# A decoder block on one NeuronCore: the transfers that form the weights' block sums move from SyncE's queue to GpSimd's

## The chip, the cores and the metric

The kernel runs on one core of one Trainium2 chip. It has five engines, each with a queue of its own that it works through in order: TensorE (PE; its weight loads are shown as PEld), VectorE (DVE), ScalarE (ACT), GpSimd (POOL) and SyncE (SP). Transfers are started by an instruction in the queue of SP, ACT or POOL; the 16 DMA engines of the core then carry them out. An instruction waits on semaphores at the head of its queue, and whatever stands behind it in that queue waits with it.

The metric is the device time of one launch in microseconds, the median of the runs.

## What is computed

The reference is one decoder block: conditioning from `c`, a combined input projection, a chunked gMLP branch and a sparse-attention branch, gates, an output projection, then a SwiGLU feed-forward layer and a final RMSNorm. The change touches the feed-forward layer:

```python
mod = jax.nn.silu(c) @ w_ada + b_ada
shift1, scale1, gate1, shift2, scale2, gate2 = [m[:, None, :] for m in jnp.split(mod, 6, axis=-1)]
...
h2 = rms_norm(x, norm2_g) * (1.0 + scale2) + shift2
f_g, f_u = jnp.split(h2 @ w_ffn_in, 2, axis=-1)
x = x + gate2 * ((jax.nn.silu(f_g) * f_u) @ w_ffn_out)
```

512 positions, a model width of 1024, a hidden width of 2816, all in float32.

## The kernel before

A float32 product is made of three TensorE products of high and low parts (`mm3`, L51). High parts come from ScalarE, low parts from VectorE as the difference. So each weight block that arrives from device memory costs work on both engines before TensorE can use it.

The two feed-forward projections use Strassen's scheme in Winograd's form: a product of 2x2 blocks takes seven block products, with sums and differences of blocks on both sides. For the first projection (`w_ffn_in`) the sums are made on chip, by VectorE. For the second (`w_ffn_out`) the sums of weight blocks are made in device memory by the DMA engines: four tensors `wsum1` to `wsum4`, each of 1280 x 512, hold them (L274). A sum is formed by a plain copy of one block into `wsum` and then an accumulating transfer that adds another block to it. `wsum_steps` (L292) makes the steps. The rows are cut in five row blocks of 256 (`NZ = 5`), and for each of them there are six steps in a chain:

1. copy a block into wsum1 and another into wsum3 (two transfers);
2. add a block to wsum1 and another to wsum3 (two transfers);
3. copy wsum1 into wsum2;
4. add a block to wsum2;
5. copy wsum2 into wsum4;
6. add a block to wsum4.

Each transfer has 512 KB. In all there are 20 plain copies and 20 accumulating ones. Before the change the plain ones are issued from SP (L307), the accumulating ones from POOL (L305), since only that queue is used for accumulation. Row blocks 0 and 1 are interleaved step by step, then 2 and 3, and block 4 comes alone.

The first projection is a loop over 20 iterations, q from -2 to 17 (L1623), with 84 matmuls of 128x256 each. `s_issue(q + 2)` (L1626) puts two loads of `w_ffn_in` (tile `raw`, L1298) into SP's queue, two iterations ahead; their buffers are those of earlier loads, so SP waits there until VectorE has read the old content. `s_prep(q + 1)` splits and sums the blocks of the next iteration on ScalarE and VectorE (L1324 to L1355). `wstep()` is called twice in each iteration (L1669, L1697) and emits the next entry of the list of steps, or nothing where the entry is None. There are 40 such calls; the list has 24 steps for row blocks 0 to 3 without a gap and then the six of block 4 with a None after each, 36 entries.

In iterations q = 1 to 8, `last_mod` (L1522) forms gate2 beside all this: in each odd one, two slices of `w_ada` (tile `mraw`, L205) are loaded on SP's queue behind that iteration's raw loads, into a pair of buffers that VectorE has just finished with; at the end of each iteration VectorE multiplies and adds one of them into `acc` (L175, L177). VectorE works in order, so what it has to do for the next iteration stands behind that instruction.

POOL has the load of gate2's bias (`gate2b`, L1470) ahead of the loop. The next thing behind the accumulating transfers is the load of the final norm's gain (`fng`, L1774), in the second projection, and at the end four small row statistics (L1235).

The second projection (`zprod`, L1732) reads weight blocks through SP (L92): blocks of `w_ffn_out` for the first product, then wsum1, wsum2, blocks of `w_ffn_out`, wsum3, wsum4 and again `w_ffn_out`. A read of wsum waits for the transfer that completed it.

The order within each engine's queue is the order of the program text (`manual_schedule`, L34); a framework adds the semaphores where one instruction needs another's result.

Of the kernel before, what the change touches and what calls it, by code (L numbers as in the profile page):

```python
# [28 lines left out]
def block_kernel(ctx: ExitStack, tc: tile.TileContext, x, positions, w_ada, b_ada, w_in,  # L29
# [3 lines left out]
    T, V, A, P, SY = nc.tensor, nc.vector, nc.scalar, nc.gpsimd, nc.sync  # L33
# [240 lines left out]
    wsum = {n: dram.tile([NZ * 256, 512], F32, name=f"wsum{n}") for n in (1, 2, 3, 4)}  # L274
# [17 lines left out]
    def wsum_steps():  # L292

        def step(c, *moves):
            o = slice(256 * c, 256 * c + 256)

            def fn():
                for n, add, src in moves:
                    if isinstance(src, tuple):
                        k = KZ[src[0]][2 * c] * 128  # L300
                        src = w_ffn_out[k:k + 256, 512 * src[1]:512 * src[1] + 512]
                    else:
                        src = wsum[src][o]
                    if add:
                        P.dma_start(wsum[n][o], src, accum_op=OP.add)  # L305
                    else:
                        SY.dma_start(wsum[n][o], src)  # L307
            return fn

        parts = [[step(c, *m) for m in (  # L310
            ((1, 0, (0, 0)), (3, 0, (0, 1))), ((1, 1, (0, 1)), (3, 1, (1, 1))), ((2, 0, 1),), ((2, 1, (1, 1)),),
            ((4, 0, 2),), ((4, 1, (1, 0)),))] for c in range(NZ)]
        return ([fn for c in (0, 2) for two in zip(parts[c], parts[c + 1]) for fn in two] +
                [fn for one in parts[4] for fn in (one, None)])

    wsteps = wsum_steps()

    def wstep():
# [1268 lines left out]
    for half in range(2):  # L1587
        o = slice(half * 256, (half + 1) * 256)
# [214 lines left out]
    for h in range(2):  # L1803
        hi, lo = get(W_FO[h])
        for tk in range(4):
            o = (Z[h] if tk < 2 else Z[2 + h])[tk % 2]
# [31 lines left out]
    for tk in range(2):  # L1838
        for z in range(2) if tk else (None,):
            c = ALL if z is None else slice(256 * z, 256 * z + 256)  # L1840
            o = Z[1][0] if z is None else (Z[1][1][:, :256], last[:, :256])[z]
            for n_, w in enumerate(ch):
                zmm(o, "S4", 2 + n_, tk, w, c, False, n_ == 2)
            n = c.stop - c.start
# [62 lines left out]
```

## Time and profile before

| | |
|---|---|
| median of 3 runs | 831.83 us (831.74 to 833.28) |
| profiled execution | 831.31 us |
| its span | 829.5 us |
| mean granted TensorE clock | 0.996 |
| TensorE busy | 810.3 us, 98% |
| VectorE busy | 684.5 us, 83% |
| DMA, mean over the span | 167 GB/s |

The span runs from the first to the last instruction; the execution's time holds a little more around it. Busy time of PE is that of pipelined matmuls with modelled ends, so in a stretch without waits it is 100% and says little; the number of matmuls that start in a window of 10 us says more. "q1" is the ring of SP's transfers, "q0" that of POOL's. The DMA share is the mean busy share of the 16 DMA engines and can pass 1 where packets of two rings overlap. "us to landing" runs from the issue of a transfer to its completion.

### The profile page before, as it was taken

The page shows a single profiled execution, that of the slowest core. Times are in us where ns is not written, and L with a number is a line of the kernel's source. Part 1 is how long each engine was busy: PE and PEld are TensorE (multiplying, and loading weights), DVE is VectorE, ACT ScalarE, POOL GpSimd, SP SyncE. Part 2 cuts the span into 40 slices and gives each one's busy share as a digit, 9 for nine tenths or more (in the row PEclk, how much of TensorE's full clock was granted, in tenths as well). Part 3 has the DMA queues.
Part 4 walks back from the last instruction along what each step waited for, and adds up shares of the span by engine and source line. Part 5 has one row for each costly group of instructions (what it writes and reads, how often), then busy time and mean ns, then how long its engine had stood idle before and what let it go on. Part 6 is the DMA issues. An engine that isn't in the chain of part 4 may idle for free.

```text
span 829.5 us, 12872 instructions
## 1 busy us (share of the span) xinstructions
PE 810.3 (98%) x4920; PEld 723.6 (87%) x4920; DVE 684.5 (83%) x1167; ACT 427.0 (51%) x730; POOL 126.7 (15%) x121
## 2 busy tenths in 40 slices
PE   7999999999999999999999999999899999999995
PEld 6889889988888888988888899999899999888784
DVE  7989788798899558886697869899699888897676
ACT  6674444323322236665536586555355556666543
POOL 2060032362353411000000001001000000000001
PEclk9999999999999999999999999999999999999999
DMA  9974352423345652057531409899998863556533
GB/s 296 310 203 118 102 178 77 118 87 101 124 137 176 197 178 77 26 157 243 185 102 50 154 28 257 222 271 295 254 265 208 199 162 125 178 189 195 177 129 126
DMA packets 108477, 138.46 MB, mean 167 GB/s; under 512 B 6480, under 2 KB 77136, under 8 KB 108256
## 3 DMA queue, kind: packets, MB, share of 16 engines
q1 hardware_dynamic: 99872, 120.24, 45.7%
q0 software_dynamic: 7824, 16.59, 10.4%
q8 instruction: 38, 0.62, 0.3%
q10 hardware_dynamic: 720, 0.82, 0.3%
q14 instruction: 23, 0.19, 0.1%
HBM read 135.26 MB, written 23.07 MB: 191 GB/s over the span
## 4 chain that ended last, share of the span: by engine, by line
PE 50%; DVE 18%; DMA 6%; ACT 2%; issue 2%; POOL 0%; POOLq 0%; ACTq 0%; DVEq 0%
PE R L53 6%; PE R L54 6%; PE R L55 6%; DMA mraw<-in_w_ada_dram 6%; PE pfo L55 3%; PE pfo L53 3%; PE pfo L54 3%; DVE acc L177 3%; DVE sco L713 2%; DVE m L709 2%; PE pb L53 2%; PE pb L55 2%; PE pb L54 2%; DVE lo L116 2%; PE po L54 2%
## 5 line engine op out<-in xcount | busy, mean ns | idle before, releaser
L112 ACT ACTIVATE hi<-raw 128x1024 fp32r<-128x1024 f32 (+2 forms) x103 | 107.0, 1040 | 105.3 <-PE pfo L55 34.3
L116 DVE TENSOR_TENSOR lo<-raw,hi 128x1024 fp32r<-128x1024 f32 (+2 forms) x67 | 81.1, 1214 | 29.1 <-ACT hi L112 28.9
L116 POOL TENSOR_TENSOR lo<-raw,hi 128x1024 fp32r<-128x1024 f32 x29 | 73.3, 2531 | 127.9 <-ACT hi L112 122.2
L53 PE MATMUL pb<-h,hi 128*128 128x512 f32 (+1 forms) x192 | 74.6, 389 | 0.0
L54 PE MATMUL pb<-h,hi 128*128 128x512 f32 (+1 forms) x192 | 74.0, 385 | 0.0
L55 PE MATMUL pb<-h,lo 128*128 128x512 f32 (+1 forms) x192 | 74.0, 385 | 0.0
L54 PE MATMUL pfo<-lo,za 128*128 128x512 f32 (+1 forms) x146 | 56.3, 385 | 0.3 <-DVE lo L116 0.3
L55 PE MATMUL pfo<-hi,za 128*128 128x512 f32 (+1 forms) x146 | 56.2, 385 | 0.0
L53 PE MATMUL pfo<-hi,za 128*128 128x512 f32 (+1 forms) x146 | 56.1, 385 | 0.0
L177 DVE SCALAR_TENSOR_TENSOR acc<-mraw,cols,acc 128x512 f32<-128x512 f32 x49 | 39.6, 808 | 18.9 <-DMA mraw<-in_w_ada_dram 17.9
L53 PE MATMUL R<-tb,hi 128*128 128x256 f32 x160 | 45.0, 281 | 2.9 <-ACT R L1670 2.1
L53 PE MATMUL R<-tb,sx 128*128 128x256 f32 x160 | 45.3, 283 | 0.9 <-ACT R L1657 0.8
L54 PE MATMUL R<-tb,sx 128*128 128x256 f32 x160 | 45.1, 282 | 0.0
L55 PE MATMUL R<-tb,sx 128*128 128x256 f32 x160 | 45.0, 281 | 0.0
L55 PE MATMUL R<-tb,lo 128*128 128x256 f32 x160 | 44.9, 281 | 0.0
L54 PE MATMUL R<-tb,hi 128*128 128x256 f32 x160 | 44.7, 279 | 0.0
L305 POOL DMA_DIRECT2D wsum<-in_w_ffn_out_dram x20 | 17.8, 908 | 172.7 <-DMA wsum<-wsum 115.3
L55 PEld LDWEIGHTS pb<-h,lo 128*128 128x128 f32 x192 | 36.0, 187 | 7.3
L54 PEld LDWEIGHTS pb<-h,hi 128*128 128x128 f32 x192 | 36.0, 188 | 6.9
L53 PEld LDWEIGHTS pb<-h,hi 128*128 128x128 f32 x192 | 36.0, 188 | 6.9
L1235 POOL TENSOR_TENSOR sm<-sm,mhalf 128x1 f32<-128x1 f32 x8 | 5.3, 662 | 217.6 <-DVE sm L1234 217.6
L54 PE MATMUL pav<-lo,h 128*128 128x256 f32 x128 | 35.8, 279 | 0.0
(373 smaller groups left out, 2643.6 us busy)
## 6 DMA issues: line engine op xcount, KB each, us to landing
raw<-in_w_ffn_in_dram SPq DMA_DIRECT2D x44, 512.0 KB, 6.5
raw<-in_w_in_dram SPq DMA_DIRECT2D x40, 512.0 KB, 3.8
mraw<-in_w_ada_dram SPq DMA_DIRECT2D x28, 512.0 KB, 4.0
wsum<-in_w_ffn_out_dram POOLq DMA_DIRECT2D x20, 512.0 KB, 9.3
raw<-wsum SPq DMA_DIRECT2D x20, 512.0 KB, 3.7
raw<-in_w_ffn_out_dram SPq DMA_DIRECT2D x18, 512.0 KB, 3.8
s<-in_w_ada_dram SPq DMA_DIRECT2D x30, 256.0 KB, 5.6
wsum<-in_w_ffn_out_dram SPq DMA_DIRECT2D x10, 512.0 KB, 8.6
```

The source lines that it names most:

```text
L53: T.matmul(o, wh, rh, start=start, stop=False, **kw)
L54: T.matmul(o, wh, rlo, start=False, stop=False, **kw)
L55: T.matmul(o, wlo, rh, start=False, stop=stop, **kw)
L112: A.activation(hi[:, :m], e["raw"][:, :m], AF.Copy)
L116: e["lo"].tensor_sub(lo[:, :m], e["raw"][:, :m], f(hi[:, :m]))
L177: V.scalar_tensor_tensor(o, w, cs[:, j:j + 1], o, op0=OP.mult, op1=OP.add)
L305: P.dma_start(wsum[n][o], src, accum_op=OP.add)
L709: V.max(m8s[i], sco[i])
L713: V.match_replace(out=sco[i], in_to_replace=m8s[i], in_values=sco[i], imm_value=TAKEN)
L1235: P.tensor_tensor(r2[:, tk:tk + 1], r2[:, tk:tk + 1], mhalf[:, :1], op=OP.pow)
```

## The change

```diff
--- before.py
+++ after.py
@@ -304,14 +304,14 @@
                     if add:
                         P.dma_start(wsum[n][o], src, accum_op=OP.add)
                     else:
-                        SY.dma_start(wsum[n][o], src)
+                        P.dma_start(wsum[n][o], src)
             return fn
 
         parts = [[step(c, *m) for m in (
             ((1, 0, (0, 0)), (3, 0, (0, 1))), ((1, 1, (0, 1)), (3, 1, (1, 1))), ((2, 0, 1),), ((2, 1, (1, 1)),),
             ((4, 0, 2),), ((4, 1, (1, 0)),))] for c in range(NZ)]
-        return ([fn for c in (0, 2) for two in zip(parts[c], parts[c + 1]) for fn in two] +
-                [fn for one in parts[4] for fn in (one, None)])
+        order = [fn for c in (0, 2) for two in zip(parts[c], parts[c + 1]) for fn in two] + parts[4]
+        return [fn for k in range(0, len(order), 3) for fn in order[k:k + 3] + [None]]
 
     wsteps = wsum_steps()
```

The 20 plain copies are issued from POOL's queue, as the accumulating transfers are. The order of the steps is the same; a None now follows every third step, so that the list has 40 entries for the 40 calls of `wstep()`. The line numbers of the rest of the kernel do not move.

## The prediction

> **What bounds the kernel now.** I read the page first, then busy time in 10 us windows over the first FFN projection, then who waited for whom where the windows show a hole, then the two issue queues and the DMA engines in that stretch.
>
> ```profile
> span 829.5 us, 12872 instructions
> PE 810.3 (98%) x4920; PEld 723.6 (87%) x4920; DVE 684.5 (83%) x1167; ACT 427.0 (51%) x730; POOL 126.7 (15%) x121
> ```
>
> TensorE has work for 98% of the span, so a change that touches no matmul can only give back, or add to, the few places where TensorE stands still. The profiled execution took 831.31 us in all, 1.8 more than its span and 0.5 less than the median of the runs, 831.83. The windows have one such place in the FFN projection (columns: stretch, its length, busy time and starts of PE, PEld, DVE, ACT and POOL, granted clock, DMA share, GB/s):
>
> ```profile
> 580.00:590.00 10.00, 10.00 (x86) 9.89 (x84) 5.44 (x8) 2.84 (x6) 0.00 (x0) 1.00 1.11 234
> 590.00:600.00 10.00, 7.11 (x47) 6.72 (x47) 7.41 (x10) 3.99 (x6) 1.27 (x2) 0.83 0.81 296
> 600.00:610.00 10.00, 9.20 (x78) 9.00 (x77) 9.59 (x13) 6.45 (x12) 0.50 (x1) 1.00 1.05 221
> ```
>
> A full window, like the first, has 86 matmul starts; 590 to 610 has 47 + 78, so 47 starts are missing, at 10/86 = 0.116 us each 5.5 us. Part of it is idle, part the granted clock of 0.83. The DMA engines are full or nearly so, 0.81 to 1.11. The waits between 574 and 606 us name the cause:
>
> ```profile
> DVE acc L175 <- DMA mraw<-in_w_ada_dram: 6.4, 1, 6.4
> ACT sx L1335 <- DMA raw<-in_w_ffn_in_dram: 3.1, 1, 3.1
> PE R L53 <- ACT R L1670: 2.1, 1, 2.1
> ```
>
> VectorE stood 6.4 us for a slice of w_ada (mraw) and everything it prepares for TensorE came late. Why was that load late? These are SP's issues, then POOL's, around it (start, duration, what; "x4" is four issues):
>
> ```profile
> 497.82 2.55 SPq L307 DMA_DIRECT2D wsum<-in_w_ffn_out_dram  x4
> ...
> 532.61 2.18 SPq L1298 DMA_DIRECT2D raw<-in_w_ffn_in_dram  x2
> ...
> 542.58 2.18 SPq L1298 DMA_DIRECT2D raw<-in_w_ffn_in_dram  x2
> ...
> 553.29 1.59 SPq L1298 DMA_DIRECT2D raw<-in_w_ffn_in_dram  x2
> ...
> 562.50 2.18 SPq L1298 DMA_DIRECT2D raw<-in_w_ffn_in_dram  x2
> 564.73 3.02 SPq L307 DMA_DIRECT2D wsum<-in_w_ffn_out_dram  x4
> 573.48 1.59 SPq L1298 DMA_DIRECT2D raw<-in_w_ffn_in_dram  x2
> 576.81 1.19 SPq L205 DMA_DIRECT2D mraw<-in_w_ada_dram  x2
> ...
> 602.92 1.03 SPq L205 DMA_DIRECT2D mraw<-in_w_ada_dram  x2
> ```
>
> ```profile
> 487.11 0.57 POOL L1470 DMA_DIRECT2D gate2b<-in_b_ada_dram  x1
> 506.75 1.93 POOL L305 DMA_DIRECT2D wsum<-in_w_ffn_out_dram  x2 [19.07 <-DMA wsum<-in_w_ffn_out_dram]
> ...
> 572.97 0.88 POOL L305 DMA_DIRECT2D wsum<-in_w_ffn_out_dram  x1 [18.22 <-DMA wsum<-in_w_ffn_out_dram]
> ...
> 577.18 0.88 POOL L305 DMA_DIRECT2D wsum<-in_w_ffn_out_dram  x1 [0.42 <-issue]
> ...
> 677.25 0.88 POOL L305 DMA_DIRECT2D wsum<-in_w_ffn_out_dram  x1 [19.24 <-DMA wsum<-wsum]
> ```
>
> SP's queue is paced by compute: a raw load waits for VectorE to free its buffer, so SP passes two iterations in 562.50 - 542.58 = 19.9 us, and the plain copies of wsum, standing between the loads, are paced with them. Each second iteration from q=1 to q=7 has a burst of four loads, two raw and two mraw. At 573 four accumulating transfers started together with such a burst. The issues between 572 and 578 us, with median time to landing, show who lost:
>
> ```profile
> wsum<-in_w_ffn_out_dram POOLq DMA_DIRECT2D x4, 512.0 KB, 11.2
> raw<-in_w_ffn_in_dram SPq DMA_DIRECT2D x2, 512.0 KB, 13.8
> mraw<-in_w_ada_dram SPq DMA_DIRECT2D x2, 512.0 KB, 16.1
> ```
>
> **The change, part by part.** What the steps are and what they depend on stays. Twenty plain copies leave SP's queue and join POOL's; empty slots are spread through the list of steps. No instruction on TensorE, VectorE or ScalarE moves.
>
> *The even spread: nothing.* A slot of the list sets only where a step stands in its queue, and a queue is paced only by waits. In the order of the changed kernel POOL's 40 issues of wsum stand in one row between gate2b and fng, and wait for nothing but landings of transfers of POOL's own queue. Nothing there waits for TensorE, VectorE or SP. So POOL runs through all of them at the pace of their landings, from gate2b at 487.7 us on. The pacing of SP is lost, not gained.
>
> *What the wsum transfers cost the DMA engines.* Queues and issues between 490 and 700 us:
>
> ```profile
> q1 hardware_dynamic: 25326, 35.19, 49.5%
> q0 software_dynamic: 5458, 10.53, 32.2%
> ...
> raw<-in_w_ffn_in_dram SPq DMA_DIRECT2D x37, 512.0 KB, 6.6
> wsum<-in_w_ffn_out_dram POOLq DMA_DIRECT2D x20, 512.0 KB, 9.3
> wsum<-in_w_ffn_out_dram SPq DMA_DIRECT2D x10, 512.0 KB, 8.6
> wsum<-wsum SPq DMA_DIRECT2D x10, 512.0 KB, 7.1
> mraw<-in_w_ada_dram SPq DMA_DIRECT2D x8, 512.0 KB, 10.3
> raw<-in_w_ffn_out_dram SPq DMA_DIRECT2D x3, 512.0 KB, 3.6
> ```
>
> q0 is POOL's: 0.322 x 210 us / 20 = 3.4 us of all engines for an accumulating transfer. q1 is SP's: 0.495 x 210 / 68 issues = 1.5 us for a plain one. The whole wsum work is 20 x 3.4 + 20 x 1.5 = 98 us, the same before and after.
>
> *Over how long it is spread.* Before: 497.8 to 677.25 + 9.3 = 686.6, 189 us, a share of 0.52. After: three blocks (two pairs of column blocks and a single one), each with six steps in a chain, copy, add, copy, add, copy, add, so by the median landings 8.6 + 9.3 + 7.1 + 9.3 + 7.1 + 9.3 = 50.7 us a block, 152 us in all, done at about 640. The share becomes 98/152 = 0.64. A plain copy from POOL's queue into device memory does not occur before; I take SP's landing times for it. Bounds from the extremes of the two lines:
>
> ```profile
> L307 SPq DMA_DIRECT2D wsum<-wsum x10: 473/522/3041, 524.9 to 671.0; - x10
> ...
> DMA to landing us min/median/max: 5.5/8.2/10.7
> ...
> L305 POOL DMA_DIRECT2D wsum<-in_w_ffn_out_dram x20: 872/881/1307, 506.8 to 677.3; - x20
> ...
> DMA to landing us min/median/max: 6.6/9.3/14.9
> ```
>
> All at minimum: 3 x (3 x 5.5 + 3 x 6.6) = 109 us, share 0.90. All at maximum: 3 x (3 x 10.7 + 3 x 14.9) = 230 us, share 0.43. I take the medians: they were measured beside the same loads.
>
> *What meets it.* In the stretch with mraw loads two iterations carry four raw and two mraw loads, 6 x 1.5 = 9.1 us in 19.9, a share of 0.46. Before: 0.52 + 0.46 = 0.98, just full, which is why one bad coincidence cost 6.4 us. After: 0.64 + 0.46 = 1.10. The stretch runs from the first burst at 532.6 to the last mraw's landing, 602.92 + 10.3 = 613, and the chain covers all of it: 80 us x (0.64 - 0.52) = 9.6 us more work than the engines have time for. Who waits for it? In the rows of 572 to 578 the additions kept their pace and the loads took the delay. So the loads wait, VectorE waits for them, and I book the whole 9.6 us there, in pieces at the four bursts, the largest where the four additions of the second block stand (about 488 + 51 + 9 = 548 to 560 us, on the burst of about 553).
>
> The Trainium skill, "DMA: Bandwidth & Descriptors", section "Queues, rings and completion order", says that each DMA engine takes turns between the queue rows with work, a packet at a time. That speaks against the change: a copy that stood in line with SP's loads now competes with them from another row. The rows of 572 to 578 agree, as far as loads losing to additions go; whether plain copies from POOL press as hard, no row here shows.
>
> *From VectorE to TensorE.* 6.4 us of waiting became 5.5 us lost, so the slack between them is 0.9 us and the wait of before has used it. From there each us passes through: the loss becomes 5.5 + 9.6 = 15.1 us.
>
> *SP's side: nothing.* SP is freed of twenty issues, at 473 to 3041 ns each. Its loads wait for buffers that VectorE frees, and a load behind a copy had an iteration, 10 us, to land. Even 1 us gained per burst would not undo an overload. Without that cover the gain is bounded by the copies' share of a burst's wait, which is rival A.
>
> *POOL's side: nothing.* Twenty more issues at 881 ns, 18 us, on an engine idle until the load of fng:
>
> ```profile
> 709.93 0.58 POOL L1774 DMA_DIRECT2D fng<-in_final_norm_g_dram  x1 [31.79 <-PE R L55]
> 711.09 8.30 SPq L92 DMA_DIRECT2D raw<-wsum  x3
> ```
>
> Behind the waiting additions stand only further additions, then fng, then row statistics of the end. The first sum is read at 711.09; with the chain at its longest (488 + 230 = 718) only the fourth sum would be late, and that is read last of the four. Were this cover gone, SP would stand before that read and TensorE with it.
>
> *Sum:* 831.3 + 9.6 = 840.9 on the profiled execution; the median lies 0.5 above it. The engines cannot be overbooked for long without the landings, and so the chain, stretching; for that I take a little off: 840 us.
>
> **The rivals.** A, *the coincidence goes* (faster). Before, additions start at 572.97 and a burst at 573.48 because both follow SP's rhythm; a free chain may miss the bursts, or slow itself down (by maximum landings its share falls to 0.43). Then the 5.5 us come back: 831.3 - 5.5 = 825.8. Against it: a chain with a share of 0.64 leaves no burst alone. The Trainium skill, "SBUF — State Buffer", section "SBUF: two separate sides", has another way to a slow chain: VectorE in certain modes locks POOL out of writing descriptors. In the quoted line 20 issues took 872 to 1307 ns beside a busy VectorE, so no run here shows such a lock.
>
> B, *only the issuer changes* (no change): all transfers share the same engines, the chain stretches by as much as it is pressed, and the waiting stays near 6 us: 831.5. For it: the work of 98 us is the same. Against: the share of 0.98 before. The same page on DMA, section "Issuing engines are not separate DMA queues", of the Trainium skill says that issuing from several engines saves no more than issue time; by that alone nothing would change, but here the queue also set the pace.
>
> C, *the chain runs at its shortest* (slower still): share 0.90, for 109 us from 488 to 597, over the bursts from 532.6 to 597: 64 us x (0.90 - 0.52) = 24 us, less the 16 us x 0.52 = 8 that the rest of the stretch is spared, so 16 more: 847. For it: two column blocks run side by side, so a stage can start before the last landing of the one before. Against: minimum landings are those of an idle machine.
>
> That the change does not do what it says, an even spread, is my forecast itself.
>
> **How the numbers follow.** Forecast 0.60, C 0.13, A 0.19, B 0.08. About 0.2% (1.7 us) is what a measurement of this kernel can tell from no change. Slower holds the forecast and C, 0.73; faster is A, 0.19; same is B, 0.08. The time is the forecast's, 840. The range must leave out no more than 2 in 10: 827 to 848 takes in B and C and the upper edge of A. The forecast's own range is 835 to 846: half the overload to one and a half times it.
>
> **What would show it.** Right: no wsum issue on SP; POOL's first at about 488 and its last before 650; VectorE's waits for mraw at three or four bursts, together 12 to 18 us; missing matmul starts in several windows between 540 and 615, none after; from 660 on the DMA share lower than before. Wrong: POOL's issues reaching past 690 (something paces them), waits for mraw under 6 us (A), loads landing in 9 us beside four additions (the engines do not favour POOL's), or TensorE waiting after 711 for a wsum load.

## The result, and the profile after

The changed kernel takes 838.22 us (median of 4 executions, 837.22 to 839.22), the kernel before 831.91 us beside it (4 executions, 831.74 to 833.28): a ratio of 1.0072, with a 95% interval of 1.0055 to 1.0090. It is slower by 6.3 us; 840 had been forecast. The profiled execution took 839.22 us.

First the head of the page of the changed kernel:

```profile
span 837.4 us, 12858 instructions
...
PE 812.6 (97%) x4920; PEld 725.5 (87%) x4920; DVE 685.0 (82%) x1167; ACT 426.3 (51%) x730; POOL 136.8 (16%) x141
```

The same 4920 matmuls in a span that is 7.9 us longer: TensorE stands still more. Where, the windows over the first FFN projection show (stretch, its length, busy time and starts of PE, PEld, DVE, ACT and POOL, granted clock, DMA share, GB/s):

```profile
540.00:550.00 10.00, 10.00 (x87) 10.00 (x85) 5.55 (x9) 4.11 (x8) 2.68 (x3) 1.00 1.05 348
550.00:560.00 10.00, 4.96 (x34) 4.66 (x34) 6.53 (x9) 2.32 (x5) 1.41 (x2) 0.81 1.11 235
560.00:570.00 10.00, 8.00 (x54) 7.60 (x53) 3.72 (x6) 2.65 (x8) 2.03 (x3) 0.85 1.02 334
570.00:580.00 10.00, 8.65 (x73) 8.66 (x74) 9.79 (x14) 5.80 (x9) 0.80 (x2) 1.00 1.03 233
580.00:590.00 10.00, 9.52 (x80) 9.32 (x80) 9.90 (x15) 5.62 (x13) 3.47 (x5) 1.00 0.85 209
...
600.00:610.00 10.00, 8.55 (x72) 8.35 (x71) 8.30 (x11) 3.99 (x6) 1.41 (x2) 1.00 1.12 284
610.00:620.00 10.00, 9.19 (x77) 8.99 (x76) 9.55 (x14) 6.34 (x12) 0.87 (x1) 1.00 0.96 275
```

Against 86.5 starts in a full window (86 or 87 in the windows shown as full), the six short ones have 34 + 54 + 73 + 80 + 72 + 77 = 390 where 519 would be full: 129 missing, at 0.116 us 14.9 us. Before it was 5.5 us in two windows. The waits of the changed kernel between 495 and 715 us (who waited, for what: us in total, times, longest) say what stood behind it:

```profile
DVE acc L175 <- DMA mraw<-in_w_ada_dram: 10.5, 2, 7.1
...
DVE raw L1327 <- DMA raw<-in_w_ffn_in_dram: 8.2, 3, 6.3
...
PE R L53 <- ACT ps L1677: 6.5, 2, 5.0
...
ACT hi L1335 <- DMA raw<-in_w_ffn_in_dram: 3.8, 1, 3.8
...
PE R L53 <- ACT R L1670: 2.6, 1, 2.6
...
PE R L53 <- ACT R L1657: 2.0, 3, 0.8
```

TensorE waited 6.5 + 2.6 + 2.0 = 11.1 us. In windows of 1 us the granted clock was 0.50 behind its longest wait, until 563 us, and TensorE worked for 4.7 us of that: 4.7 x (1 - 0.50) = 2.4 us more. Together 13.5 of the 14.9 us; the rest was not followed. Above TensorE's waits stand VectorE and ScalarE waiting for loads, and not for mraw alone: the raw loads of `w_ffn_in` were as late. In the kernel before VectorE waited 6.7 us for mraw in this stretch and for no raw load.

The first matmul of the second projection tells how late the loop ended. One row from the view of the tile pfo in the changed kernel (duration min/median/max in ns, first and last start):

```profile
L53 PE MATMUL pfo<-hi,za x146: 277/395/400, 720.0 to 829.4; 128*128 128x512 f32 x134, 128*128 128x256 f32 x12
```

Before, the same row goes from 710.9 to 820.3. The loop ends 9.1 us later, and the whole second projection is shifted by the same 9.1 us. The span grows by 7.9 only: the tail behind the last of these matmuls is 829.5 - 820.3 = 9.2 us before and 837.4 - 829.4 = 8.0 after. That 1.2 us goes with the queue: the tail is 9.2 us in all four kernels here that leave the copies on SP, and 7.9 to 8.1 in the six that have them on POOL with sums and whole pieces (changed, paced, one and five blocks at a time, mraw loaded once, a wait between pairs). In the two kernels that leave the sums out it is 10.5 and 10.7, so the queue is not all of it; what it is stays open.

Now the queue. The transfers of wsum in the changed kernel (issue time in ns, first and last start):

```profile
L305 POOL DMA_DIRECT2D wsum<-in_w_ffn_out_dram x20: 869/894/985, 494.5 to 627.1; - x20
...
L307 POOL DMA_DIRECT2D wsum<-in_w_ffn_out_dram x10: 557/894/914, 487.6 to 587.7; - x10
L307 POOL DMA_DIRECT2D wsum<-wsum x10: 505/518/529, 502.2 to 621.7; - x10
```

All 40 are POOL's, from 487.6 to 627.1 where they had gone to 677.3. Nothing of the list's even spread shows in them. POOL's issues where the first pair of row blocks ends and the second begins (the last addition of blocks 0 and 1, four copies of blocks 2 and 3, then the first and the last of four additions):

```profile
532.19 0.89 POOL L305 DMA_DIRECT2D wsum<-in_w_ffn_out_dram  x1 [1.66 <-DMA wsum<-wsum]
532.76 2.58 POOL L307 DMA_DIRECT2D wsum<-in_w_ffn_out_dram  x4
543.71 0.92 POOL L305 DMA_DIRECT2D wsum<-in_w_ffn_out_dram  x1 [8.37 <-DMA wsum<-in_w_ffn_out_dram]
...
550.79 0.89 POOL L305 DMA_DIRECT2D wsum<-in_w_ffn_out_dram  x1 [0.92 <-DMA wsum<-in_w_ffn_out_dram]
```

and SP's issues in the same stretch:

```profile
532.57 2.17 SPq L1298 DMA_DIRECT2D raw<-in_w_ffn_in_dram  x2
534.79 2.30 SPq L205 DMA_DIRECT2D mraw<-in_w_ada_dram  x2
542.53 19.51 SPq L1298 DMA_DIRECT2D raw<-in_w_ffn_in_dram  x4
```

The first step of blocks 2 and 3 waits for nothing of blocks 0 and 1, so it starts while the last additions of these are still moving: a seam at which POOL's ring holds ten transfers almost without a pause. The burst of 532.6 to 535 meets the first half of it, the two raw loads behind 542.53 the second. In the view of the DMA issues between 542 and 546 us (KB, median us to landing), and of the rings between 548 and 562 us (packets, MB, share of 16 engines' time):

```profile
raw<-in_w_ffn_in_dram SPq DMA_DIRECT2D x2, 512.0 KB, 23.8
```

```profile
q0 software_dynamic: 1038, 2.14, 79.1%
q1 hardware_dynamic: 1072, 1.33, 32.4%
```

A raw load took 23.8 us here, against 6.6 in the median before and 13.8 for the two at the hole of before. And the two rings moved nearly the same number of packets, the pieces in which the profile counts what a ring moves, 1038 and 1072: the engines serve them in turn, one packet each. POOL's packet (q0) takes 0.791 x 16 x 14 us / 1038 = 171 ns, SP's (q1) 0.324 x 224 / 1072 = 68 ns. So while both rings were filled, SP's ring had less than a third of the time: 1.33 MB in 14 us, one load of 0.524 MB in 5.5 us. The loop needs one in 3.3 us where mraw is loaded (six in 19.9 us) and one in 5 us elsewhere.

### The profile page after: what moved, and what is told of

Read it like the earlier page. It is cut to its first block, busy times and chain, and to the rows that moved or that the text cites. A ratio compares the mean times of both kernels' runs of the same rounds, so it can differ in the third digit from the quotient of the medians.

```text
span 837.4 us, 12858 instructions
## 1 busy us (share of the span) xinstructions
PE 812.6 (97%) x4920; PEld 725.5 (87%) x4920; DVE 685.0 (82%) x1167; ACT 426.3 (51%) x730; POOL 136.8 (16%) x141
## 4 chain that ended last, share of the span: by engine, by line
PE 83%; DVE 6%; DMA 6%; ACT 2%; issue 1%; SPq 0%; POOL 0%; POOLq 0%; DVEq 0%
PE pb L53 9%; PE pb L55 9%; PE pb L54 9%; PE R L53 5%; PE R L54 5%; PE R L55 5%; PE pfo L55 3%; PE pfo L53 3%; PE pfo L54 3%; DMA raw<-in_w_ffn_in_dram 3%; PE pav L54 2%; PE pav L53 2%; PE pav L55 2%; PE pgb L53 2%; PE pgb L54 2%; PE pgb L55 2%
## 5 line engine op out<-in xcount | busy, mean ns | idle before, releaser
L53 PEld LDWEIGHTS R<-tb,hi 128*128 128x128 f32 x160 | 30.7, 192 | 7.0 <-ACT ps L1677 6.9
```

What stands on the lines that cost most here:

```text
L53: T.matmul(o, wh, rh, start=start, stop=False, **kw)
```

## The experiments

All times are medians, each compared with the kernel before on the same chip; over the chips used, the median of the kernel before lay between 831.2 and 832.1. Edits are shown against the changed kernel where nothing else is said. "Loop end" is the first start of pfo as above, from the profiled execution; for a wait between pairs and for no additions that execution lay 2.4 and 2.7 us above the median, so their loop ends are late by about as much.

| run | us | ratio to before, 95% interval | loop end |
|---|---|---|---|
| before | 831.9 | | 710.9 |
| changed | 838.22 | 1.0072 [1.0055, 1.0090] | 720.0 |
| list alone | 833.47 | 1.0019 [1.0009, 1.0030] | 712.3 |
| paced by ScalarE | 827.33 | 0.9966 [0.9934, 0.9997] | 706.2 |
| one block at a time | 824.39 | 0.9914 [0.9892, 0.9936] | 705.8 |
| mraw loaded once | 837.13 | 1.0073 [1.0051, 1.0094] | 717.7 |
| five blocks at once | 861.41 | 1.0364 [1.0340, 1.0388] | 741.7 |
| a wait between pairs | 831.92 | 1.0004 [0.9989, 1.0018] | 715.1 |
| one at a time, copies on SP | 830.18 | 0.9978 [0.9963, 0.9994] | 707.8 |
| mraw earlier, kernel before | 837.35 | 1.0070 [1.0052, 1.0088] | 716.2 |
| no additions | 832.51 | 1.0010 [0.9994, 1.0027] | 713.6 |
| five at once, no additions | 855.36 | 1.0283 [1.0234, 1.0333] | 734.1 |
| short pieces | 1219.33 | 1.4653 [1.4627, 1.4680] | 719.2 |
| five at once, short pieces | 1216.72 | 1.4634 [1.4612, 1.4656] | 720.9 |

### The list alone, the copies left on SP

```diff
-                        P.dma_start(wsum[n][o], src)
+                        SY.dma_start(wsum[n][o], src)
```

> The new list with its even gaps, plain copies left on SP. Theory (the loss comes from the wsum work losing SP's pace and being pressed into 147 us over the mraw bursts): the copies keep SP's pace, the chain even ends some 20 us later than before, so no loss: 827 to 832 us. Rival (the even list itself is what hurts): near 838. Rival (the ring the copies come from is what hurts): also 827 to 832, so this run does not tell the ring from the pace.

1.5 us slower than before. It keeps one hole, later than that of before; its window, and the wait behind it:

```profile
610.00:620.00 10.00, 5.76 (x36) 5.48 (x36) 6.38 (x9) 3.18 (x6) 0.00 (x0) 0.83 0.67 247
```

```profile
DVE acc L177 <- DMA mraw<-in_w_ada_dram: 7.4, 1, 7.4
```

So the list moves the coincidence to another burst and does not remove it. The other half, the old list with the copies on POOL, would be the changed kernel itself: POOL issues nothing between its 40 transfers of wsum, and the two lists have them in the same order. The loss is that of the queue.

### On POOL, but paced

```diff
         fn = wsteps.pop(0) if wsteps else None
         if fn:
+            mark = ffn[0].tile([128, 1], F32, name="mark", tag=f"mark{len(wsteps)}", bufs=1)
+            seen = ffn[0].tile([128, 1], F32, name="seen", tag="seen", bufs=1)
+            A.activation(mark, f(onesr[:, 0:1]), AF.Copy)
+            P.tensor_tensor(seen, mark, mhalf[:, :1], op=OP.pow)
             fn()
```

> As the changed kernel, all wsum transfers on POOL, but in front of each step POOL waits for a one-column ScalarE instruction of that iteration, so the steps really are spread over the 20 iterations. Theory (pace): wsum's share of the DMA engines falls from 0.67 to about 0.5, the additions no longer overlap in fours, VectorE's waits for mraw under 4 us together: 826 to 832 us. Rival (ring: plain copies from POOL's ring press SP's loads whatever their pace): still 836 to 840.

827.33 us, with executions from 825.2 to 828.2 and three at 833.9 to 834.7; the profiled one, 825.49, is of the first kind. The issues of wsum now run from 509.8 to 703.3, and VectorE waits 3.1 us for loads where it had waited 18.7. All copies are POOL's here too, so POOL's ring as such does not cost: what it had lost was the pace.

### One row block at a time

```diff
-        order = [fn for c in (0, 2) for two in zip(parts[c], parts[c + 1]) for fn in two] + parts[4]
+        order = [fn for one in parts for fn in one]
```

> As the changed kernel, all wsum transfers on POOL and without any wait for compute, but the five row blocks one after another, not two interleaved. Theory (how much wsum work stands in the DMA engines at a time): the chain takes 5 x 40 to 50 = 200 to 250 us, a share of 0.4 to 0.5, at most two additions at once: 826 to 831 us, faster than before. Rival (ring): 836 to 840, since every copy still comes from POOL. Rival (phase, only the coincidence of bursts with additions counts): anything from 826 to 838.

824.39 us: this beats both kernels, by 0.9% and 1.6%. It has no added wait; a chain of dependent transfers leaves pauses by itself. Its additions, its windows at the place of the changed kernel's hole, and the rings between 532 and 566 us:

```profile
L305 POOL DMA_DIRECT2D wsum<-in_w_ffn_out_dram x20: 869/890/982, 493.8 to 668.0; - x20
```

```profile
550.00:560.00 10.00, 10.00 (x87) 10.00 (x86) 9.57 (x12) 6.53 (x13) 2.55 (x4) 1.00 0.72 223
560.00:570.00 10.00, 10.00 (x86) 10.00 (x86) 9.24 (x16) 4.50 (x9) 0.91 (x1) 1.00 1.05 320
```

```profile
q0 software_dynamic: 1207, 3.56, 47.4%
q1 hardware_dynamic: 4214, 5.18, 45.3%
```

The same two rings in the changed kernel, same stretch:

```profile
q0 software_dynamic: 2202, 5.72, 72.0%
q1 hardware_dynamic: 3253, 3.75, 35.6%
```

SP's loads need six times 0.524 MB in 19.9 us, 5.4 MB in these 34 us. One block at a time lets through 5.18, the changed kernel 3.75. Over the whole chain, though, POOL's share here is that of the kernel before: 98 us of work in the 188 us from 487.7 to the last landing at about 675, 0.52. A mean share cannot tell these apart. That only the phase counts, which transfer happens to meet which burst, is not excluded by this run alone.

### mraw loaded once

```diff
-        if k % 2 == 0:
+        if k == 0:
```

Here six of the eight mraw loads are left out; VectorE multiplies the first two slices again.

> As the changed kernel, but only the first two of the eight mraw slices of w_ada are loaded and all eight multiply-adds read those two: six loads and the right value of gate2 are left out. Theory (overload in the stretch with mraw loads): 0.67 + 0.31 leaves the engines just not full, most of the loss goes: 827 to 832 us. Rival (the raw loads of w_ffn_in are hurt as much, mraw is only the messenger): 834 or more, with VectorE and ScalarE waiting for raw.

837.13 us: the loss stays although six of the 24 loads of that stretch are gone. Two windows and the first two of VectorE's waits for loads:

```profile
550.00:560.00 10.00, 5.87 (x37) 5.67 (x38) 7.69 (x10) 2.66 (x4) 1.66 (x3) 0.77 1.11 238
560.00:570.00 10.00, 7.03 (x50) 6.77 (x48) 3.96 (x8) 3.66 (x8) 2.30 (x3) 0.84 1.04 305
```

```profile
DVE raw L1327 <- DMA raw<-in_w_ffn_in_dram: 9.7, 3, 6.0
...
DVE acc L175 <- DMA mraw<-in_w_ada_dram: 6.4, 1, 6.4
```

The later, smaller holes of 600 to 620 are gone, and the big one stands. By the prediction's arithmetic the engines are no longer full without those loads, 0.64 + 4 x 1.5 / 19.9 = 0.94; so an overload of the whole stretch with mraw loads is not the mechanism. The first mraw burst is still there, and VectorE's 6.4 us are a wait for it, so its part in the big hole stays open in this run; in the next run the loss begins before any mraw load.

### All five row blocks at once

```diff
-        order = [fn for c in (0, 2) for two in zip(parts[c], parts[c + 1]) for fn in two] + parts[4]
+        order = [fn for same in zip(*parts) for fn in same]
```

> As the changed kernel, but all five row blocks side by side: ten copies, then ten additions, then five of each and five of each again. Theory (what counts is how much wsum work stands in POOL's ring without a pause, against the 10 to 13 us that a load has to land): 10 x 1.5 + 10 x 3.4 = 49 us without a pause from 488 on; the loads land one in about 7 us while two are needed in 10; 845 to 860 us, and the loss lies at 505 to 590, much of it before the first mraw load at 535. Rival (only the stretch with mraw loads can be hurt): the chain is nearly done when that stretch begins, 828 to 838.

861.41 us. The windows from 500 us on have 82, 73 and 32 starts, so the loss begins long before the first mraw load of this kernel at 545. Rings and raw loads between 500 and 540 us:

```profile
q0 software_dynamic: 3078, 7.02, 82.1%
q1 hardware_dynamic: 3015, 3.01, 26.8%
...
raw<-in_w_ffn_in_dram SPq DMA_DIRECT2D x4, 512.0 KB, 18.7
```

Again nearly equal numbers of packets (310 and 310 between 512 and 516 us alone), 171 ns for POOL's (0.821 x 640 / 3078) and 57 ns for SP's. 3.01 MB in 40 us is one load in 7.0 us, where the loop needs one in 5 even without mraw. This run gave the rule its plain form: not how much POOL moves counts, but how long its ring is never empty.

### A wait between the pairs

```diff
+        def after_landing(c, fn):
+            def both():
+                t = ffn[0].tile([128, 1], F32, name="seen", tag="seen", bufs=1)
+                P.dma_start(t, wsum[4][256 * c:256 * c + 128, 0:1])
+                fn()
+            return both
+
+        parts[2][0], parts[4][0] = after_landing(1, parts[2][0]), after_landing(3, parts[4][0])
```

> As the changed kernel, but between two pairs of row blocks POOL waits until the last addition of the pair has landed (it issues a 512-byte read of wsum4 in between). The chain gets some 15 us longer, 162 instead of 147. Theory (standing work): the ten transfers that stood together at 530 to 566 (two additions, four copies, four additions, 26 us) become at most eight, 20 us: the loss falls to a half or less, 829 to 834 us. Rival (mean share of the DMA engines, the sum of the prediction): 98/162 = 0.60 instead of 0.67, 835 to 838.

831.92 us, 6.3 us better than the changed kernel for two reads of 512 bytes whose only use is to hold POOL until the earlier pair has landed. One hole remains, 20 us later, from four copies at 545.4 and the four additions behind them, on the burst of 553:

```profile
570.00:580.00 10.00, 5.17 (x27) 4.97 (x26) 3.41 (x6) 1.33 (x2) 2.30 (x3) 0.66 1.03 315
580.00:590.00 10.00, 7.95 (x65) 7.54 (x65) 9.90 (x13) 6.94 (x13) 1.94 (x3) 1.00 0.92 239
```

Against one block at a time, 824.39, the changed kernel loses 13.8 us, and the two waits at the seams take back 6.3 of them. The rest belongs to two blocks side by side. That the loss is about halved and no more is what the account by standing work had expected, and not that by mean shares.

### One block at a time, copies on SP

```diff
-                        P.dma_start(wsum[n][o], src)
+                        SY.dma_start(wsum[n][o], src)
```

This is against the run of one block at a time.

> The row blocks one after another, as in the kernel that came to 824 us, but with the plain copies on SP as before. Theory: the standing work is as small, but a copy on SP that depends on an addition now waits at the head of SP's queue, and the raw loads behind it with it, some 3 to 8 us in many iterations: 828 to 842 us, slower than with POOL. Rival (only the order of the row blocks counts): 823 to 827.

830.18 us, 5.8 us more than with the copies on POOL. Between the two profiled executions, 829.81 and 825.0, 2.0 us lie in the loop (707.8 against 705.8) and 1.2 in the tail (9.2 against 8.0); the rest comes in the second projection, which waits for loads that it has at once in the other kernel. Its waits from 700 us on:

```profile
ACT hi L112 <- DMA raw<-in_w_ffn_out_dram: 7.8, 3, 5.9
ACT hi L112 <- DMA raw<-wsum: 7.4, 6, 2.6
```

A copy that waits at the head of SP's queue for the landing of an addition holds up every load behind it: SP stood so nine times, 57.7 us in all, between 490 and 715 us. The last copy left at 696.3, and the four loads of `w_ffn_out` behind it only then; in the other kernel the first of those four left at 693.6. The first read of wsum left at 713.8, there at 706.1. That this makes the waits of the second projection is likely, but not shown. The queue, which costs 6 us with two blocks side by side, gains 6 with one.

### mraw issued earlier, in the kernel before

This one is against the kernel before, and asks whether its own hole goes when the load that was late has more time:

```diff
-        if k % 2 == 0:
+        if k == 0:
...
-                mgl[k + e][0](mgr[e])
+                mgl[e][0](mgr[e])
...
+        if k + 2 < 8:
+            mgl[k + 2][0](mgr[k % 2])
```

> The kernel before, with each mraw load issued two iterations ahead of its use (as soon as its own half of the buffer is free) instead of one. If the 5.5 us that the kernel before loses at 590 hang on mraw's 9.4 us of time to land: 826 to 828 us. If the raw loads beside it would have held TensorE up anyway: 829 to 832.

837.35 us, a miss by every theory that had been written down. The mraw load now reuses a buffer that VectorE has not finished with, and stands at the head of SP's queue until it has. SP's waits between 490 and 640 us, and ScalarE's:

```profile
SPq L205 <- DVE acc L177: 41.4, 6, 12.6
```

```profile
ACT sa L1324 <- DMA raw<-in_w_ffn_in_dram: 17.6, 4, 8.4
```

In the kernel before, the first of these waits adds up to 5.0 us. An earlier issue in the program text became a later issue of the raw loads behind it.

### No additions

What about an accumulating transfer presses so hard? This run makes the twenty additions plain copies, so that the sums are left out; by the prediction's estimates a copy takes 1.5 us of the engines and an addition 3.4:

```diff
-                        P.dma_start(wsum[n][o], src, accum_op=OP.add)
+                        P.dma_start(wsum[n][o], src)
```

> The changed kernel, but the twenty accumulating transfers are plain copies from the same source to the same place, from the same queue, in the same order (what was summed before is left out: only the last copied block stands in each wsum). Theory (what counts is the work of the engines that stands in POOL's ring without a pause, 3.4 us for an accumulating transfer and 1.5 us for a plain one): the seam of the two pairs shrinks from about 26 us of work to 10 x 1.5 = 15 us, and the whole chain from 98 to 60 us; no hole of more than a few matmul starts, 823 to 827 us. Rival (a ring beside SP's takes turns by the transfer or the packet, so the number of POOL's transfers counts and not their kind): the raw loads of the seam still land after 20 us and more, 834 to 840 us.

> All five row blocks side by side, as in the run that took 861 us, with plain copies in place of the accumulating transfers (sums left out in the same way). Theory of engine work: 60 us of work that stands without a pause, with eight transfers in flight at once, 8 x 1.5 = 12 us ahead of a load instead of up to 27: the first bursts from 500 us on may lose a few us, the end comes soon (chain over in 70 to 90 us); 824 to 832 us. Rival by the number of transfers: eight in flight press as before, 845 to 861 us.

832.51 and 855.36 us. Both are far from what the theory of engine work gives (823 to 827, 824 to 832); the second is where the rival had it, the first between the two. With five at once, the rings between 500 and 540 us:

```profile
q0 software_dynamic: 2404, 10.79, 75.7%
q1 hardware_dynamic: 3279, 3.26, 24.8%
...
raw<-in_w_ffn_in_dram SPq DMA_DIRECT2D x4, 512.0 KB, 26.4
```

POOL's packets are 10.79 / 2404 = 4.5 KB here in the mean, against 7.02 / 3078 = 2.3 KB with additions, and take 0.757 x 640 / 2404 = 202 ns. A whole copy is cheaper than an addition (between 486 and 576 us all forty took 63 us of the engines, 1.6 each), but its turn is not shorter, and the turn is what each packet of SP has to wait out. The counts are not equal over these 40 us, though. They are while POOL copies from `w_ffn_out` (345 against 347 between 512 and 516 us, packets of 3.7 KB in 146 ns); while it copies from wsum to wsum, in packets of 12.9 KB and 611 ns, there were 91 against 230 between 528 and 532. So one packet each is not the whole rule, and SP's ring got no more there: 0.22 MB in 4 us. SP's 3.26 MB in 40 us are one load in 6.4 us. What less work buys is only that the ring is empty sooner: the last wsum issue is at 558 and not at 578. "Engine work that stands ahead", the theory of the runs up to here, was thus not right either; what fits all runs up to here is the time that POOL's ring stays filled.

### Short pieces

If a turn is a packet, smaller packets on POOL's side should help the loads. The edit walks each transfer as two column halves, once in the changed kernel and once with five at once:

```diff
+                    to, src = (t.rearrange("r (b c) -> b r c", c=256) for t in (wsum[n][o], src))
                     if add:
-                        P.dma_start(wsum[n][o], src, accum_op=OP.add)
+                        P.dma_start(to, src, accum_op=OP.add)
                     else:
-                        P.dma_start(wsum[n][o], src)
+                        P.dma_start(to, src)
```

> The changed kernel with every transfer of wsum (copies and additions) walked as two column halves, so that its contiguous pieces are 1 KB as those of a raw load are; instructions, order and bytes stay. New theory (the DMA engines take one packet of each ring in turn; in the run of five at once, 500 to 540 us, q0 had 3078 packets of 171 ns and q1 3015 of 57 ns, so a raw load of 512 packets on 16 engines took 32 x (171 + 57) = 7.3 us, one load per 7 us, while a ring of POOL stood): pieces of 1 KB need more packets on POOL's side and each takes less, 75 to 100 ns, so a load needs 32 x (57 + 75 to 100) = 4.2 to 5 us; the queue of loads of the changed kernel's seam does not form or is halved: 824 to 833 us, raw loads under 15 us. Rival (loads lose by the number of transfers or by the bytes that stand ahead, however they are cut): 835 to 840 us, raw loads over 20 us as in the changed kernel.

> Five row blocks side by side, as in the run of 861 us, with the same halving of the contiguous pieces. New theory: with POOL's ring always full a load needs 4.2 to 5 us in place of 7.3, where an iteration of 10 us needs two or four of them: most of the loss of 29 us goes, 830 to 845 us; the count of q0's packets in 500 to 540 us at least twice 3015 less what the two rings have equal, both rings about equal in number. Rival by transfers or bytes: 855 to 865 us.

1219 and 1217 us, nowhere near. The transfers themselves became several times as long; rings of the first of the two between 510 and 550 us, and the wait that makes its time:

```profile
q1 hardware_dynamic: 4717, 5.19, 41.2%
q0 software_dynamic: 4382, 0.88, 15.9%
```

```profile
ACT hi L112 <- DMA raw<-wsum: 392.8, 13, 165.5
```

An addition took some 40 us, the last one was issued at 1145, and the second projection stood 393 us for the sums. As a test of the whole time it failed, and it is none of the turns either. The 4382 packets are of two kinds: 3692 of some 65 bytes between 514 and 522 us, and behind them, up to 546 us, only 54 to 101 of about 1 KB in each 4 us, which took 8 to 12% of the engines. So POOL's ring was not filled for most of that time, and SP's 5.19 MB are no more than the ten loads that it issued there. What kept POOL's ring so slow was not followed. The loop ends at 719.2, as late as in the changed kernel, with many small waits for one big one; with five at once it ends at 720.9, where it had been 741.7.

## Why the prediction held, and which step did not

*Size and sign.* 840 forecast, 838.22 measured. The loss in the loop was to be 5.5 + 9.6 = 15.1 us; it is 14.9.

*"The even spread: nothing."* Shown: POOL's issues run from 487.6, and an order built with the old list is the same. The list does act where the copies stay on SP, by 1.5 us.

*The cost of the wsum work*, 98 us. The rings of the changed kernel between 490 and 700 us:

```profile
q0 software_dynamic: 7235, 21.06, 43.5%
```

0.435 x 210 = 91 us, a little under the estimate; of the forty, only the first four were issued a little before that stretch, at 487.6.

*Over how long.* 152 us forecast, done at about 640; the last issue is at 627.1, so with a landing of some 7 us 634, 147 us. The plain copies landed from POOL's queue in 8.0 us in the median, where they had taken 8.2 from SP's, as assumed; the slowest took 15.8 against 10.7.

*The overload: the step that failed.* The prediction multiplied a difference of mean shares, 0.64 - 0.52, by the 80 us of the mraw stretch, and booked all of it as VectorE's wait for mraw at three or four bursts, 12 to 18 us. The runs contradict the mechanism three times: one block at a time has the share of 0.52 and no hole to speak of, where the kernel before with 0.52 has one; with six mraw loads left out the loss stays; with five at once it begins before any mraw load. VectorE's measured waits for mraw are 10.5 us at two bursts, and it waits 8.2 us for raw loads, which the step did not foresee; ScalarE's waits for raw loads are what they were (7.2 against 7.1). In its place: as long as POOL's ring is not empty, SP's packets wait their turn behind POOL's, and SP's ring gives one load in 5.5 to 7 us instead of the 3.3 to 5 that the loop takes. The loss goes with the longest stretch without a pause, and the pairs make one at the seam. That the sum came out so well is in part luck: the seam falls where the overload was placed, on the burst of about 553, but nothing in the step sets how long it lasts.

The Trainium skill, "DMA: Bandwidth & Descriptors", section "Queues, rings and completion order", has the rule that was needed: an engine "round-robins between the queue rows it has work for, at *packet* granularity". The runs agree, with 1038 packets against 1072 and 3078 against 3015 where both rings were full; they do not where POOL copied from wsum to wsum, 91 against 230. The prediction used the rule for the direction only, and the profile before held the price: at its own hole, between 581 and 589 us, POOL's ring moved 596 packets of 171 ns and SP's 600 of 64 ns, and SP's 0.68 MB in these 8 us are one load in 6.2 us.

*From VectorE to TensorE, one to one.* Not quite: VectorE's waits for loads grew by 12.0 us (18.7 against 6.7), TensorE's loss by 9.4 (14.9 against 5.5). More waiting than was booked, of which less came through: that the two nearly cancel is luck too.

*SP's side: nothing.* Not so. In the changed kernel the tail is 1.2 us shorter than before, as in the other five kernels named with it above, and with one block at a time, taking the copies off SP is worth 5.8 us (824.39 against 830.18). So this step was a term of its own, set to zero; whether more than the 1.2 us lies hidden under the loss of the changed kernel, no run shows. The section "Issuing engines are not separate DMA queues" of the same page of the Trainium skill says that issuing from several engines saves no more than issue time; here the same 20 copies cost 6.3 us with two blocks side by side and gain 5.8 with one, for reasons of pace and of what waits at a queue's head, which that sentence does not speak of.

*POOL's side: nothing.* Right: behind the last wsum issue POOL stood idle until fng.

*The rivals.* A, the coincidence goes, is what one block at a time does: 824.39, near its 825.8. It needed another order of the steps, which the change does not make. B, only the issuer changes, would hold if the queue did nothing but issue; the two runs that differ in the queue alone, by 5.8 us, speak against it. C, the chain at its shortest, is surpassed by five at once.

## What to carry to other kernels

When transfers move to another queue, count not their bytes or their mean share but how long that queue's ring will stay filled without a pause, and divide: with two rings filled, the engines alternated here, mostly packet by packet, and the loads that compute waits for got the share that their packet size gave them. Background work belongs in a chain of dependent transfers, one after the other, on a queue where nothing urgent stands behind it; interleaving two independent chains to hide their landings is what starved the loads here. One chain gives 824.39 us, 0.9914 of the kernel before [0.9892, 0.9936].

## What the runs showed of the hardware that was not expected

A plain copy inside device memory presses a load beside it as hard as an accumulating transfer of twice its engine time: with five blocks at once, SP's ring moved 3.26 MB in 40 us beside copies and 3.01 MB beside copies and additions. That fits turns by packet, since the packets of the copies alone were twice as large (4.5 KB in 202 ns against 2.3 KB in 171 ns).

With five blocks at once POOL issued eight transfers in 4.45 us and the ninth only after a landing, as the later ones did; whether chip or framework sets that number was not tried.

Walking the transfers of wsum by column halves made one addition last about 40 us where it had taken about 10; for more than half of that time POOL's ring moved no more than 54 to 101 packets of about 1 KB in each 4 us.
